# Two tiles for the high and the low part of every moving operand of the feed-forwards, the low ones at another place in a 256-byte line

## The chip, the cores and the metric

One core of one Trainium2 chip runs the whole program. The time is device microseconds from start to end of the program. A profile beside it records one execution: when each engine (PE for matrix multiplies, PEld for loading their weights, DVE and ACT for elementwise work, POOL, and SP, which here issues transfers) was busy and what ended each wait.

## The reference

Two layers of a diffusion backbone over 512 latent tokens and 256 context tokens, model width 1024. Layer 0 mixes tokens by windowed attention, layer 1 by retention; after each mixer comes a SwiGLU feed-forward of inner width 2816, modulated and gated by columns made from a condition vector. In layer 1 only the latent tokens go through the feed-forward. Cut to what matters here:

```python
D_MODEL = 1024; SEQ = 512; CTX_LEN = 256
D_FF = -(-8 * D_MODEL // (3 * 256)) * 256

def swiglu(h, w_in, w_out):
    gate, up = jnp.split(h @ w_in, 2, axis=-1)
    return (jax.nn.silu(gate) * up) @ w_out

    for i in range(DEPTH):
        mx = jnp.split(c_act @ ada_w[i] + ada_b[i], 6, axis=-1)
        mc = jnp.split(cc_act @ ada_w[i] + ada_b[i], 6, axis=-1)
        ...  # the mixer, with its gated residual
        x = x + mx[5] * swiglu(modulate(rms_norm(x, norm2_g[i]), mx[3], mx[4]), ffn_w_in[i], ffn_w_out[i])
        if need_ctx_out:
            y_ctx = y_ctx + mc[5] * swiglu(modulate(rms_norm(y_ctx, norm2_g[i]), mc[3], mc[4]),
                                           ffn_w_in[i], ffn_w_out[i])
```

## The kernel before

**Tokens lie along the columns.** A tile has 128 partitions, which hold 128 of the 1024 features, and its columns are tokens. Weights are the stationary operand of a matmul, tokens or activations the moving one.

**Every matmul comes in threes.** A 32-bit value is split into a high part, rounded by a cast on ACT (`fp32r`), and a low part, the rest, by a subtraction on DVE (`split`, L164). A product is then the sum of three matmuls into the same PSUM tile: weights high times tokens high, weights low times tokens high, weights high times tokens low. `mm3` (L144) issues them at L148, L149 and L150; `product` (L902) does the same in a loop at L908. So one matmul in three reads the low part of a moving tile.

**Layer 0's feed-forward** (L923 to L1157) treats 512 latent and 256 context tokens as 768, in two halves of 384 columns (`THIRDS`). It runs over 22 blocks of 128 inner features. The first two (`first_two`, `plain`) multiply each half by the gate and the up weights, 8 steps of `mm3` each. The other 20 (`seven`, L1025) use a Strassen-like scheme: seven products of 4 steps, each 384 columns wide, on sums of halves made once (`token_sums`, `last_sum`). Blocks are gathered in groups of 2, 4, 4, 4, 4, 4 (`FFN_GROUPS`), and after the first block of the next group `output` (L1078) multiplies the group's activations by the output weights: for each of 8 output tiles one sum over the latent tokens (512 columns, PSUM tile pj) and one over the context tokens (256 columns, PSUM tile Z).

The moving tiles are `aq` (768 columns: high part first, low part behind it, 384 each; 8 in pool `ep`, 20 in pool `hq`) and `act` (1536 columns: 768 high, 768 low; 5 in `ep`). `parts` (L927) cuts an `aq` in two. Before the first use, the `act` tiles hold the unsplit tokens (`tm`), two per tile. Of the 20 `aq` tiles in `hq`, 12 serve for a short while as room for weight blocks of 512 columns: `unit` (L1107) loads two blocks of modulation weights, `unit(10)` and `unit(11)`, each as 8 transfers of 512 columns (four of the second go to another tile, `crow`), and `ada_unit` (L302) multiplies them at L308 in pieces of 128 columns. After that `token_sums` fills the same tiles with the sums of halves.

**Layer 1's feed-forward** (L1610 to L1723) has 512 latent tokens in two halves of 256 columns. The first three blocks are plain, the other 19 go through its own `seven` with seven products of 4 steps, 256 columns wide. Moving tiles: `hx` (the tokens, 8 high and 8 low, allocated in turn in pool `hX`), `sA` (sums of halves, likewise, pool `fp`), both 512 columns, and `ax` (activations, 512 columns, in turn, 10 in pool `fa`), which `output` (L1686) reads whole, 512 columns per matmul, 8 output tiles x 22 blocks.

**Where a tile starts in a 256-byte line.** Nearly all tiles have a multiple of 64 columns (256 bytes), so they start at byte 0 of a line, but the program shifts some with a small padding tile: `off_grid(pool, cols)` (L225) allocates `cols` columns of 4 bytes in the pool and clears them on POOL. 16 columns shift what follows by 64 bytes, 48 by 192. Worked out from the sizes of the tiles that stand ahead, the starts are:

| moving tile | columns read | before, high / low | after, high / low |
|---|---|---|---|
| aq (layer 0) | 384 | 0 / 0 | 0 / 64 |
| act (layer 0) | 512 and 256 | 0 / 0 | 0 / 64 |
| hx, sA (layer 1) | 256 | 64 / 64 | 64 / 192 |
| ax (layer 1) | 512 | 0 / 0 | 0 / 192 |
| h (layer 0's mixer) | 512 | 0 / 0 | the same |
| hc (layer 0's mixer, context) | 256 | 192 / 192 | the same |
| qk, wx, aq, hc, sA in layer 1's mixer | 256, 512 | 0 / 0 | the same |

The weights (`whi`, `wlo` and the tiles that stand in for them) start at byte 0 of a line in both feed-forwards, before and after.

**What sets the order.** Instructions stand on each engine in an order that a planner chooses from the program as written, its dependencies and its own costs; each engine then works through its list in order. SP issues nearly all transfers, weights above all, one after the other, and a transfer into a tile waits until the tile's last reader is done. Tiles of one tag take turns in their buffers.

## Time and profile before

| | |
|---|---|
| time, median of 3 runs | 1767.8 us (1767.19 to 1768.53) |
| the profiled execution | 1765.14 us |
| its span, first to last instruction | 1763.4 us |
| mean granted TensorE clock | 0.996 of full speed |
| PE busy | 1716.5 us, 97% of the span |
| DVE busy | 1332.7 us, 76% |
| ACT busy | 841.3 us, 48% |
| layer 0's feed-forward, by the chain | from about 375 to 900 us |
| layer 1's feed-forward | from about 1409 us to the end |

How to read it: busy times are unions of the instructions' intervals, and those of PE are modelled at their ends: neighbouring matmuls overlap in the record (a 256-column matmul has a duration of about 0.28 us and starts 0.12 us after the one before). The distance between starts is what a stream of matmuls costs. The chain of waits merges neighbours on one line into one row, with start, length and count, and so gives that distance. Names are those of the program with buffer numbers left out: `Y<-aq,whi` is a matmul into PSUM tile Y that reads moving tile aq and weights whi.

### The profile page before, as it was taken

To read this page: it belongs to the slowest core of one execution; us is meant where nothing else is said; L and a number is where in the kernel's file an instruction comes from. 1 tells how busy PE (TensorE), PEld (TensorE's weight loads), DVE (VectorE), ACT (ScalarE), POOL (GpSimd) and SP (SyncE) were. 2 spreads that over 40 slices of the span, in tenths; PEclk is the share of its full clock that TensorE was granted. 3 is DMA by queue.
4 is the path that set the end of the run, shared out by engine and by line. 5 is a ranking of instruction groups with operands and counts; after the bars stand their busy time and mean duration, and the time that the engine had idled before them with its cause. 6 is when DMAs were issued, how large, how long until landed. Compare 5 with 4: busy or idle time off the path is not lost.

```text
span 1763.4 us, 27889 instructions
## 1 busy us (share of the span) xinstructions
PE 1716.5 (97%) x10984; PEld 1531.5 (87%) x10984; DVE 1332.7 (76%) x2342; ACT 841.3 (48%) x1487; POOL 122.4 (7%) x267
## 2 busy tenths in 40 slices
PE   6999999999999999999998999999999999999999
PEld 4788787889999999999887888898897889989998
DVE  6687786478778787877799758758767897777774
ACT  5467786364434333343464534524534565345442
POOL 0014344000000000000010000000000100000000
PEclk9999999999999999999999999999999999999999
DMA  9510014133243434343333434434433323233322
GB/s 345 232 49 14 15 58 157 49 127 113 96 132 122 142 120 155 108 145 130 96 133 120 157 98 132 155 108 133 146 105 108 96 93 111 85 108 108 97 83 84
DMA packets 60899, 205.65 MB, mean 117 GB/s; under 512 B 6752, under 2 KB 7136, under 8 KB 60640
## 3 DMA queue, kind: packets, MB, share of 16 engines
q1 hardware_dynamic: 53856, 178.71, 30.5%
q0 software_dynamic: 6912, 25.17, 4.5%
q8 instruction: 86, 1.41, 0.3%
q14 instruction: 45, 0.37, 0.1%
HBM read 201.75 MB, written 2.10 MB: 116 GB/s over the span
## 4 chain that ended last, share of the span: by engine, by line
PE 78%; DVE 12%; DMA 5%; ACT 3%; issue 1%; POOL 0%; SPq 0%; DVEq 0%; ACTq 0%; POOLq 0%
PE Y L908 14%; PE Z L908 7%; PE pj L150 7%; PE pj L149 7%; PE pj L148 7%; DMA wraw<-in_wst_dram 4%; PE X L908 3%; PE Y L1253 3%; PE Z L1266 3%; DVE wlo L166 3%; PE pO L732 2%; PE pT L704 2%; PE S L684 2%; PE pj L1266 2%; PE X L1253 1%
## 5 line engine op out<-in xcount | busy, mean ns | idle before, releaser
L165 ACT CAST whi<-wraw 128x1024 fp32r<-128x1024 f32 x177 | 185.5, 1051 | 305.2 <-PE Z L150 71.5
L166 DVE TENSOR_TENSOR wlo<-wraw,whi 128x1024 fp32r<-128x1024 f32 x177 | 216.1, 1223 | 39.4 <-ACT whi L165 38.9
L908 PE MATMUL Y<-aq,whi 128*128 128x384 f32 x640 | 173.9, 335 | 0.4 <-ACT hn L1046 0.3
L253 DVE SCALAR_TENSOR_TENSOR res<-pj,mod,res 128x512 f32<-128x512 f32 (+1 forms) x110 | 80.4, 732 | 81.2 <-PE pj L150 80.1
L141 DVE TENSOR_TENSOR wlo<-wraw,whi 128x1024 fp32r<-128x1024 f32 x79 | 96.5, 1223 | 35.2 <-ACT whi L140 34.6
L140 ACT CAST whi<-wraw 128x1024 fp32r<-128x1024 f32 x79 | 82.9, 1049 | 77.1 <-PE Z L150 24.3
L908 PEld LDWEIGHTS Y<-aq,whi 128*128 128x128 f32 x640 | 116.7, 188 | 1.8 <-ACT hn L1046 1.4
L908 PE MATMUL Y<-aq,wlo 128*128 128x384 f32 x320 | 107.0, 334 | 0.0
L271 DVE CUSTOM_DVE_ANT_0 y<-adaw,crow,small_sb 128x1024 bf16<-128x1024 f32 x64 | 81.9, 1280 | 32.9 <-DMA adaw<-in_adaT_dram 32.7
L1266 PE MATMUL Z<-whi,sA 128*128 128x512 f32 x256 | 81.0, 392 | 1.4 <-ACT whi L165 1.4
L101 ACT ACTIVATE pr<-pr,stat,qs 128x513 f32<-128x513 f32 (+2 forms) x96 | 74.2, 775 | 12.4 <-DVE stat L691 9.7
L698 POOL TENSOR_SCALAR pr<-pr,stat 128x512 f32<-128x512 f32 (+2 forms) x96 | 65.3, 693 | 76.6 <-DVE stat L695 57.7
L148 PE MATMUL pj<-ax,whi 128*128 128x512 f32 x176 | 68.7, 390 | 1.2 <-DVE res L253 1.2
L150 PE MATMUL pj<-ax,whi 128*128 128x512 f32 x176 | 68.7, 390 | 0.0
L149 PE MATMUL pj<-ax,wlo 128*128 128x512 f32 x176 | 68.5, 389 | 0.0
L148 PE MATMUL pj<-act,whi 128*128 128x512 f32 x168 | 66.0, 393 | 0.0
L149 PE MATMUL pj<-act,wlo 128*128 128x512 f32 x168 | 65.9, 392 | 0.0
L150 PE MATMUL pj<-act,whi 128*128 128x512 f32 x168 | 65.5, 390 | 0.0
L268 POOL DMA_DIRECT2D adaw<-in_adaT_dram x48 | 25.6, 533 | 514.6 <-DVE mod L271 420.1
L908 PE MATMUL Y<-sA,whi 128*128 128x256 f32 x304 | 60.8, 282 | 0.0
L908 PEld LDWEIGHTS Y<-aq,wlo 128*128 128x128 f32 x320 | 60.1, 188 | 0.0
L685 DVE CUSTOM_DVE_ANT_0 pr<-S,mask,qs 128x256 f32<-128x256 f32 (+1 forms) x96 | 52.5, 568 | 8.4 <-PE S L684 5.1
(545 smaller groups left out, 5227.8 us busy)
## 6 DMA issues: line engine op xcount, KB each, us to landing
wraw<-in_wst_dram SPq DMA_DIRECT2D x238, 512.0 KB, 3.6
adaw<-in_adaT_dram POOLq DMA_DIRECT2D x48, 512.0 KB, 3.8
wx<-in_wst_dram SPq DMA_DIRECT2D x24, 512.0 KB, 4.9
adan<-in_adaQ_dram SPq DMA_DIRECT2D x16, 512.0 KB, 8.4
adan<-in_adaN_dram SPq DMA_DIRECT2D x16, 512.0 KB, 7.5
res<-in_xT_dram SPq DMA_DIRECT2D x16, 256.0 KB, 4.4
q<-in_adaN_dram SPq DMA_DIRECT2D x16, 256.0 KB, 3.2
aq<-in_adaN_dram SPq DMA_DIRECT2D x12, 256.0 KB, 5.9
```

The source lines that it names most:

```text
L101: ins = nc.scalar.activation(*args, **kw)
L140: nc.scalar.copy(hi, raw)
L141: nc.vector.tensor_tensor(lo, raw, hi, op=sub)
L148: nc.tensor.matmul(o, whi, xhi, start=first, stop=False)
L149: nc.tensor.matmul(o, wlo, xhi, start=False, stop=False)
L150: return nc.tensor.matmul(o, whi, xlo, start=False, stop=last)
L165: nc.scalar.copy(hi, t)
L166: return nc.vector.tensor_tensor(lo, t, hi, op=sub)
L253: return nc.vector.scalar_tensor_tensor(res[d], o, mods[l, s][:, part, d:d + 1], res[d], mult, add)
L271: after(nc.vector.tensor_tensor_reduce(junk, w, cr[:, s * 1024:(s + 1) * 1024], 1.0, sm_t[:, C_ADAB + l * 48 + j:C_ADAB + l * 48 + j + 1], ...
L908: nc.tensor.matmul(o, p, r, start=first and k + i == 0, stop=k == 3 and i == 2, skip_group_check=not first)
L1266: ins = nc.tensor.matmul(o, p, r, start=first and k + i == 0, stop=k == 3 and i == 2, skip_group_check=not first)
```

## The change

Each moving operand of the feed-forwards that was one tile, or two tiles allocated in turn, becomes two tiles with tags of their own: `aqh` and `aql`, `acth` and `actl`, `hxh` and `hxl`, `sAh` and `sAl`, `axh` and `axl`. All high tiles of a tag lie together, then comes a padding tile, then all low tiles, then a padding that completes the line. The number of buffers stays the same. What moves in the line stands in the table above: the low parts alone. A weight block that `unit` loads now spans a high tile (384 columns) and the first 128 columns of a low tile, so it takes two transfers; the function `cut` gives its four pieces to `ada_unit`. `sh2` grows from 16 to 64 columns so that it fills a line.

```diff
@@ -292,12 +292,15 @@
 
 
 
+    def cut(t):
+        return [t[:, j * P:(j + 1) * P] for j in range(4)]
+
     def unit_load(u):
         w = []
         for kk in range(4):
             w.append(T(st_p, 1024, "adan", 8))
             nc.sync.dma_start(w[kk], adaN[u, kk])
-        return [t[:, a * 512:(a + 1) * 512] for t in w for a in range(2)]
+        return [cut(t[:, a * 512:(a + 1) * 512]) for t in w for a in range(2)]
 
     def ada_unit(u, w, bank=pT, ccol=ccol):
 
@@ -305,7 +308,7 @@
         o = bank()[:, 0:P]
         for k in range(KT):
             for j in range(4):
-                nc.tensor.matmul(o[32 * j:32 * j + 32, :], ccol[:, k, :], w[k][:, j * P:(j + 1) * P],
+                nc.tensor.matmul(o[32 * j:32 * j + 32, :], ccol[:, k, :], w[k][j],
                                  start=k == 0, stop=k == KT - 1)
         rows = t_sq(P)
         nc.scalar.copy(rows, o)
@@ -795,7 +798,7 @@
     def load_streams():
         streams.extend(((0, load_stream(0)), (1, load_stream(1))))
 
-    def cut(w):
+    def cut_w(w):
         return [tuple(t[:, k * P:(k + 1) * P] for t in w) for k in range(KT)]
 
     def key_room_w():
@@ -846,7 +849,7 @@
 
     ends = []
     end = lambda: ends.pop(0)()
-    weight = lambda room=None: wo.append(room() if room else cut(next_w(ap, 1)))
+    weight = lambda room=None: wo.append(room() if room else cut_w(next_w(ap, 1)))
     steps = {}
     for g in range(NKV - 1):
         a, b = make_q(2 * g + 2), make_q(2 * g + 3)
@@ -889,7 +892,7 @@
     ep = E.enter_context(tc.tile_pool(name="ep", bufs=1, reuse_waits="tile"))
     wo_p = A.enter_context(tc.tile_pool(name="wo", bufs=1, reuse_waits="tile"))
     for wsel[0] in (0, 2, 3, 1):
-        wo.append(cut(next_w(wo_p)))
+        wo.append(cut_w(next_w(wo_p)))
     (_, xr), (_, cres) = streams
     for s, d in WO_ORDER:
         out_part(s, d, 0, KT)
@@ -923,13 +926,26 @@
     Q = ExitStack()
     hq = Q.enter_context(tc.tile_pool(name="hq", bufs=1, reuse_waits="tile", side="right"))
     fp = F.enter_context(tc.tile_pool(name="fp", bufs=1, reuse_waits="tile"))
-    quarter = lambda: T(hq, 768, "aq", 20, F32R)
-    parts = lambda t: (t[:, 0:384], t[:, 384:768])
+    def quarter(dt=F32R):
+        hi = T(hq, 384, "aqh", 20, dt)
+        if not begun:
+            off_grid(hq, 16)
+        lo = T(hq, 384, "aql", 20, dt)
+        if not begun:
+            begun.append(off_grid(hq, 48))
+        return hi, lo
+
+    begun = []
     bank = lambda n: T(psF, 512, n, 2)[:, 0:384]
-    fp32 = [T(ep, 2 * WIDE, "act", 5) for _ in range(4)]
-    tm = [fp32[k % 4][:, k // 4 * WIDE:(k // 4 + 1) * WIDE] for k in range(KT)]
-    A = {(k, 0): parts(T(ep, 768, "aq", 8, F32R)) for k in range(KT)}
-    A.update({(k, 1): parts(quarter()) for k in range(KT)})
+    tm = [T(ep, WIDE, "acth", 5) for _ in range(4)]
+    A = {(k, 0): [T(ep, 384, "aqh", 8, F32R)] for k in range(KT)}
+    off_grid(ep, 16)
+    tm += [T(ep, WIDE, "actl", 5) for _ in range(4)]
+    for k in range(KT):
+        A[k, 0].append(T(ep, 384, "aql", 8, F32R))
+    off_grid(ep, 48)
+    A[0, 1] = quarter()
+    A.update({(k, 1): quarter() for k in range(1, KT)})
 
     def latent_shape():
 
@@ -962,12 +978,12 @@
             nc.vector.tensor_tensor(t1[:, h1], t2[:, h2], t1[:, h1], op=sub)
             nc.vector.tensor_tensor(park[:, k * 384:(k + 1) * 384], t2[:, h1], t1[:, h1], op=sub)
             for n, t in ((1, t2[:, h2]), (3, t1[:, h2]), (2, t1[:, h1])):
-                S[n, k] = parts(quarter())
+                S[n, k] = quarter()
                 split(t, *S[n, k])
 
     def last_sum():
         for k in range(4):
-            S[4, k] = parts(quarter())
+            S[4, k] = quarter()
             split(park[:, k * 384:(k + 1) * 384], *S[4, k])
 
     S = {}
@@ -975,12 +991,12 @@
                **{n: (lambda k, n=n: S[n, k]) for n in (1, 2, 3, 4)}}
 
     def new_act():
-        return T(ep, 2 * WIDE, "act", 5, F32R)
+        return T(ep, WIDE, "acth", 5, F32R), T(ep, WIDE, "actl", 5, F32R)
 
     def finish_half(a, i, t, up):
         nc.vector.tensor_tensor(t, t, up, op=mult)
         c = THIRDS[i]
-        return split(t, a[:, c], a[:, c.start + WIDE:c.stop + WIDE])
+        return split(t, a[0][:, c], a[1][:, c])
 
     def project_half(w, i, tag):
         o = bank(tag)
@@ -1088,7 +1104,7 @@
             for k in range(gsz):
                 c0 = k * nd * P + (d % nd) * P
                 mm3(o, (wd[0][:, c0:c0 + P], wd[1][:, c0:c0 + P]),
-                    (acts[k][:, c], acts[k][:, c.start + WIDE:c.stop + WIDE]), k == 0, k == gsz - 1)
+                    (acts[k][0][:, c], acts[k][1][:, c]), k == 0, k == gsz - 1)
             ins = gated_add(s, 0, 5, d, o, res)
             if cr and not final and s == 0 and d % 2:
                 ada_next(ins)
@@ -1105,12 +1121,18 @@
                     one(*st, d)
 
     def unit(u):
-        w = [T(hq, 768, "aq", 20)[:, 0:512] for _ in range(KT - 4 * (u == 11))]
-        if u == 11:
-            more = T(fp, 2048, "crow", 1)
-            w += [more[:, i * 512:(i + 1) * 512] for i in range(4)]
+        more = T(fp, 2048, "crow", 1) if u == 11 else None
+        w = []
         for k in range(KT):
-            nc.sync.dma_start(w[k], adaN[u, k // 2][:, k % 2 * 512:k % 2 * 512 + 512])
+            src = adaN[u, k // 2][:, k % 2 * 512:k % 2 * 512 + 512]
+            if k >= KT - 4 and more:
+                w.append(cut(more[:, (k - 4) * 512:(k - 3) * 512]))
+                nc.sync.dma_start(more[:, (k - 4) * 512:(k - 3) * 512], src)
+                continue
+            a, b = quarter(F32)
+            nc.sync.dma_start(a, src[:, 0:384])
+            nc.sync.dma_start(b[:, 0:P], src[:, 384:512])
+            w.append([a[:, 0:P], a[:, P:2 * P], a[:, 2 * P:], b[:, 0:P]])
         return ada_unit(u, w, pj, columns)
 
     ada_q = []
@@ -1573,8 +1595,11 @@
         hW_parts = lambda: (T(hW, 1024, "whi", 2, F32R), T(hW, 1024, "wlo", 2, F32R))
         hm = [T(hM, 512, "hm", 8) for _ in range(KT)]
         off_grid(hX, 16)
-        hx = [(T(hX, 512, "hx", 16, F32R), T(hX, 512, "hx", 16, F32R)) for _ in range(KT)]
-        off_grid(hX, 48)
+        hx = [[T(hX, 512, "hxh", 8, F32R)] for _ in range(KT)]
+        off_grid(hX, 32)
+        for pair in hx:
+            pair.append(T(hX, 512, "hxl", 8, F32R))
+        off_grid(hX, 80)
         done = []
 
         def second_norm(k, c, behind=()):
@@ -1614,13 +1639,24 @@
     fp = F.enter_context(tc.tile_pool(name="fp", bufs=1, reuse_waits="tile"))
     ring += [rp, rp, hW, hW, fp, fp]
     wsel[0] = 4
-    sh2 = T(fp, 16, "sh2", 1)
-    sA = [(T(fp, 512, "sA", 16, F32R), T(fp, 512, "sA", 16, F32R)) for _ in range(KT)]
-    off_grid(fp, 48)
+    sh2 = T(fp, 64, "sh2", 1)
+    off_grid(fp, 16)
+    sA = [[T(fp, 512, "sAh", 8, F32R)] for _ in range(KT)]
+    off_grid(fp, 32)
+    for pair in sA:
+        pair.append(T(fp, 512, "sAl", 8, F32R))
+    off_grid(fp, 80)
+    begun = []
     operand_a = operands(lambda k, half: [a[:, HALVES[half]] for a in hx[k]], sA)
 
     def new_act():
-        return T(fa, 512, "ax", 10, F32R), T(fa, 512, "ax", 10, F32R)
+        hi = T(fa, 512, "axh", 5, F32R)
+        if not begun:
+            off_grid(fa, 48)
+        lo = T(fa, 512, "axl", 5, F32R)
+        if not begun:
+            begun.append(off_grid(fa, 16))
+        return hi, lo
 
     def half(i):
         return [(a[:, HALVES[i]], b[:, HALVES[i]]) for a, b in hx]
```

## The prediction

> **What bounds the kernel now.** I read the page's busy times first, then the stages of the two feed-forwards, then the chain that ended last, and there the distance from one matmul to the next. In the window view the columns are the stretch, its length, and the busy time of PE, PEld, DVE, ACT and POOL.
>
> ```profile
> span 1763.4 us, 27889 instructions
> PE 1716.5 (97%) x10984; PEld 1531.5 (87%) x10984; DVE 1332.7 (76%) x2342; ACT 841.3 (48%) x1487; POOL 122.4 (7%) x267
> ...
> 447.00:505.00 58.00, 58.00 (x336) 57.84 (x335) 43.66 (x65) 27.27 (x45) 2.65 (x5) 1.00 0.34 111
> 540.00:597.00 57.00, 57.00 (x330) 56.96 (x329) 47.63 (x72) 26.93 (x45) 4.22 (x8) 1.00 0.45 141
> 1461.00:1500.00 39.00, 38.98 (x327) 38.61 (x326) 29.60 (x41) 22.26 (x40) 0.00 (x0) 1.00 0.39 123
> 1522.00:1562.00 40.00, 39.47 (x333) 39.20 (x332) 27.37 (x39) 21.88 (x40) 0.00 (x0) 1.00 0.35 107
> ```
>
> Inside both feed-forwards (first two windows: layer 0, last two: layer 1) PE is busy without a gap at a granted clock of 1.00, and DVE, the next engine, has at least a sixth of its time free (47.63 of 57). So what a matmul costs here is the distance between the starts of two neighbours; the durations of single matmuls overlap and say nothing. The chain and the timeline give these starts (us, length, what):
>
> ```profile
> 640.62 2.08 PE Z L908 x12
> 642.70 4.16 PE Y L908 x24
> ...
> 1395.91 0.12 PE pj L149
> 1399.99 0.12 PE Y L150
> ...
> 1461.65 1.41 PE Z L908 x12
> 1468.85 2.83 PE Y L908 x24
> ...
> 321.06 0.28 PE L149 MATMUL S<-hc,wlo 128*128 128x256 f32 x1
> 323.56 0.28 PE L150 MATMUL S<-hc,whi 128*128 128x256 f32 x1
> ...
> 98.44 0.12 PE pj L148
> 100.91 0.12 PE pj L148
> ...
> 1453.57 0.23 PE pj L149
> 1461.30 0.23 PE pj L150
> ...
> 505.06 0.23 PE pj L148
> 507.14 0.23 PE pj L148
> ```
>
> I divide each stretch by its number of steps. 384 columns, moving tile at byte 0 of a line (aq): 4.16/24 = 173.3 ns. 256 columns at byte 0 (qk, 34 steps): 4.08/34 = 120.0. 256 columns at byte 64 (hx, sA): 2.83/24 = 117.9 and 1.41/12 = 117.5, so 117.8. 256 columns at byte 192 (hc) comes in two kinds: 2.50/22 = 113.6 in one run, 2.47/21 = 117.6 in another. 512 columns at byte 0 (ax, 34 steps): 7.73/34 = 227.4; right after a switch from the 384-column stream (act, 9 steps) 2.08/9 = 231.1. From 256 to 384 to 512 columns the distance grows by 53.3 and 54.1 ns, so what a matmul costs on top of its columns is about the same for all three sizes, and I carry a difference seen at 256 columns over to the others. All weights lie at byte 0 in these rows. That the three 256-column distances differ by where the moving tile starts, 120.0, 117.8 and 113.6 to 117.6, is the evidence the forecast rests on; it is one stage against another, not an experiment.
>
> **The change part by part.** No matmul is added or removed, and each keeps its shape. High tiles stay where they were (byte 0 in layer 0 and for ax, 64 for hx and sA). A third of the matmuls, those at L150 or the last of the three in a product, read the low tile, which moves.
>
> Layer 0, byte 0 to byte 64. From the loops: 20 fast products of 7x4 steps give 560 low matmuls, two plain blocks of 2x2x8 give 64, all 384 columns wide; the output sums give 22x8 = 176 at 512 and 176 at 256 columns. That is 976 low matmuls. Price: 120.0 - 117.8 = 2.2 ns each, 976 x 2.2 = 2.15 us. Ends: nothing, if the 64-byte rows are fast for a reason of their stage, and 6.4 ns each (120.0 - 113.6), 6.2 us. I take 2.2, which is the row for just this start.
>
> Layer 1, hx and sA low, byte 64 to byte 192. 19 products x 28 steps = 532, three plain blocks x 2x2x8 = 96: 628 at 256 columns. Price between 117.8 - 117.6 = 0.2 and 117.8 - 113.6 = 4.2 ns; nothing in the rows says which kind of run this will be, so half way, 2.1 ns: 1.3 us (0.1 to 2.6).
>
> Layer 1, ax low, byte 0 to byte 192. 176 at 512 columns, 120.0 - 117.6 = 2.4 to 6.4 ns, half way 4.4: 0.8 us (0.4 to 1.1).
>
> The high matmuls I price at nothing: around the two changes of moving start that the rows show (192 bytes after 0 at 98.44, 64 after 0 behind 1461.30) the distance is at once that of the new tile, so it goes with a matmul's own start. What speaks against: nowhere in this trace does the start alternate in every triple, as it will.
>
> On the other side: two transfers per weight block in the modulation units.
>
> ```profile
> 387.24 7.58 SPq L1113 DMA_DIRECT2D aq<-in_adaN_dram  x12
> 406.01 5.27 SPq L122 DMA_DIRECT2D wraw<-in_wst_dram  x3
> DMA to landing us min/median/max: 2.7/5.4/6.6
> 410.93 3.63 PE pj L308 x128
> 411.38 0.75 POOL L268 DMA_DIRECT2D adaw<-in_adaT_dram  x1 [94.53 <-PE pj L308]
> 1406.45 0.40 DVE res L1553
> 1406.85 0.39 DVE hx L243
> 1448.88 1.14 DVE wlo L166
> 1453.07 0.50 PE pj L148
> ```
>
> Twelve issues take 7.58 us on SP's queue; 24 take 15.2, so the last goes out at 402.4 and lands by 409.0, before its readers start at 410.93. Behind them on that queue stands the weight load of 406.01, still 3.6 us away. So nothing, with 1.9 us of cover; were landing as much later again as its own spread (6.6 - 2.7 = 3.9), PE would stand 2 us, once. Nine more memsets go to POOL, which has been idle for 94.5 us when its next work comes; none of them stands before anything in layer 1 that PE reads. Each new pool's padding has to wait for its space, as the tiles beside it do. Casts and subtractions write to another byte of the line: hx, at byte 64, took 0.39 us for 256 columns on DVE, an operation of the same size on res, at byte 0 of the line, 0.40, so nothing. At the start of layer 1's feed-forward, where DVE sets the pace up to 1453.07, the planner places some casts, splits and output matmuls one step earlier or later; one DVE step is 1.14 us, so I bound this by 1.1 us either way and take zero.
>
> Sum: -2.15 - 1.3 - 0.8 = -4.2 us, all on PE's path, since the windows leave no gap in which it could be lost. The profiled execution took 1765.14 us (span 1763.4 and 1.7 around it), 2.7 below the median of 1767.8. Off the median: **1763.6 us**.
>
> **A rule against it.** The rows show that 256 columns cost 113.6 to 120.0 ns with the same weights' start. The Trainium skill, "TensorE: Matmul & The Clock Gate", section "Step-by-step: what each phase is for", says that PE reads the moving tile and the weights through two independent ports, so that loading weights takes nothing from a running matmul, and gives (section "Back-to-back issue gap") a distance of columns over 2.4 GHz plus 2.5 ns, in which no address stands. By that rule the change would be worth nothing and the time 1767.8. The trace disagrees with the figure (an estimate from that page, 109.2 ns at 256 columns, stands against 113.6 to 120.0), so its rule for addresses weighs little with me.
>
> **The rivals.**
> *No effect.* The differences belong to the stages (which weights, which PSUM tile, what DVE does meanwhile), not to the start in the line. For it: the byte-192 runs are 113.6 and 117.6 at the same start. Against it: three stages with byte 64 or 192 all lie below every long run at byte 0. Time 1767.8.
> *The neighbour decides.* What costs is that the next stream begins at the same place in the line as the one before or as its weights; then both borders of every triple gain, at best down to the 113.6 row. Layer 0: 976 x 2 x 6.4 = 12.5 us; layer 1: 628 x 2 x 4.2 = 5.3 and 176 x 2 x 6.4 = 2.3. Together 20.1: 1747.7. For it: the two kinds of byte-192 runs show that more than the own start counts. Against it: long runs at one start are not the slowest there are.
> *Slower: each change of start costs.* After the switch to another stream at 505.06 the steps are 231.1 instead of 227.4, 3.7 ns more, for a while. If alternating starts keep PE in that condition, both matmuls that follow a border pay: 1,780 triples x 2 x 3.7 = 13.2 us, less the 4.2: +9.0, 1776.8. It decides from 4.2/3560 = 1.2 ns a border. Against it: at 98.44 and 1461.65 a change of start cost nothing that shows; but the switch there happens once.
>
> **How the numbers follow.** Own start decides 0.42 (range of its own 1758 to 1767, by the ends above), neighbour 0.20, no effect 0.16, slower 0.22. A fifth of a per cent, 3.5 us, is about what a measurement of this kernel can tell from no change. Of the first case I put 0.06 inside that, of no effect all but 0.01, of slower 0.01: faster 0.56, within 0.22, slower 0.22. The range 1747 to 1773 leaves out the better part of the slower case beyond half its price and a tail of the neighbour case.
>
> **What would show it.** Right: sums of 384 columns at 2.07 us for twelve instead of 2.08, 256-column sums of layer 1 at 1.39 to 1.41 instead of 1.41, everything outside the feed-forwards as it was. Neighbour: 384-column twelves near 2.03 and 1.38 in layer 1. Slower: twelves above 2.10. A PE gap before 410.9 would be the transfers. Most likely to make the forecast wrong is the high matmuls' share, which I set to zero: one nanosecond on each of the 3,560 is 3.6 us.

## The result, and the profile after

The changed kernel took 1773.31 us in the median of 20 runs, the kernel before 1768.38 us in 20 runs beside it: a ratio of 1.0024 (95% interval 1.0017 to 1.0032), slower by about 4.2 us (3.0 to 5.7). The forecast was 1763.6 us and faster; the time moved the other way and lies just above the range (1747 to 1773).

Part 1 of the page of the changed kernel:

```profile
span 1767.3 us, 27919 instructions
PE 1717.7 (97%) x10984; PEld 1529.9 (87%) x10984; DVE 1333.9 (75%) x2342; ACT 840.4 (48%) x1487; POOL 123.4 (7%) x276
```

The number of matmuls is the same; POOL has nine instructions more. The page of the profile hardly tells the two kernels apart. The profiled execution of before was 2.7 us below its median and this one, 1769.4 us, 3.9 below its own, so the spans can't be subtracted either. What can be compared are distances and single waits. The chain that ended last, changed kernel, in layer 0 (384 columns, then 512) and layer 1 (256); columns are start, length, what:

```profile
641.53 4.17 PE Y L911 x24
645.71 2.09 PE X L911 x12
...
871.81 0.23 PE pj L150
...
880.16 0.23 PE pj L150
...
1471.45 1.40 PE Z L911 x12
1472.86 2.81 PE Y L911 x24
```

The same view of the kernel before, at the 512-column rows (the others stand in the prediction):

```profile
871.90 0.23 PE pj L149
...
880.29 0.23 PE pj L150
```

384 columns: 4.17 us for 24 instead of 4.16. 256 columns of layer 1: 2.81 instead of 2.83. 512 columns: 36 steps in 8.35 us, 231.9 ns, where before 37 steps took 8.39 us, 226.8 ns. The twelves of layer 1 are as forecast for the case taken (1.39 to 1.41), those of layer 0 are not (2.07 was said); and the 512-column matmuls lost five nanoseconds here, for which the sum had no term.

The second place is the start of layer 1's feed-forward. The window view over 64.10 us from the first matmul on hx, before and after (two fences, same columns as in the prediction):

```profile
1409.70:1473.80 64.10, 60.82 (x453) 57.20 (x452) 59.80 (x101) 35.92 (x59) 1.66 (x2) 1.00 0.26 83
```

```profile
1411.93:1476.03 64.10, 58.89 (x441) 55.35 (x440) 58.34 (x97) 33.88 (x56) 3.78 (x8) 1.00 0.27 83
```

PE gets through 441 matmuls instead of 453 in the same time and is busy for 1.9 us less. POOL is the one engine that has more to do in it: 8 instructions instead of 2. Its timeline in the kernel before (start, length, what, and in brackets the idle time before it):

```profile
1405.97 0.26 POOL L227 MEMSET off<- 128x16 f32 x3
1407.44 0.79 POOL L210 TENSOR_TENSOR y<-y,sq 128x256 f32<-128x256 f32 x1 [1.22 <-ACT sq L209]
1408.68 0.83 POOL L210 TENSOR_TENSOR y<-y,sq 128x256 f32<-128x256 f32 x1 [0.45 <-ACT sq L209]
```

and in the changed one:

```profile
1408.19 0.32 POOL L227 MEMSET off<- 128x16 f32 x4
1412.16 0.34 POOL L227 MEMSET off<- 128x32 f32 x2 [3.65 <-PE Y L150]
1412.47 3.58 POOL L210 TENSOR_TENSOR y<-y,sq 128x256 f32<-128x256 f32 x4
```

Before, the clearing of the padding waits for nothing, and the four additions of the norm (L210, squares of the tokens summed over features) run one by one as ACT delivers them. After, the 32-column padding between sA's high and low tiles lies on space that PE reads until about 1412.1; its clearing waits 3.65 us, and the four additions stand behind it on POOL and run in one block. The view of ACT's waits of the changed kernel, 1400 to 1425 us, shows who pays:

```profile
ACT sq L209 <- POOL y L210: 2.1, 1, 2.1
```

The transfers of the modulation units, in the timeline of SP's queue (the first, the last, and the weight load behind them):

```profile
385.11 1.20 SPq L1133 DMA_DIRECT2D aqh<-in_adaN_dram  x2
...
396.45 0.43 SPq L1134 DMA_DIRECT2D aql<-in_adaN_dram  x1
403.88 5.41 SPq L122 DMA_DIRECT2D wraw<-in_wst_dram  x3
```

24 issues take 11.8 us where 12 took 7.58, and the weight load behind them goes out 7 us after the last of them. They cost nothing that can be seen.

### The profile page after: what moved, and what is told of

It is laid out like the page before. It is cut to its first block, busy times and chain, and to the rows that moved or that the text cites. A ratio compares the mean times of both kernels' runs of the same rounds, so it can differ in the third digit from the quotient of the medians.

```text
span 1767.3 us, 27919 instructions
## 1 busy us (share of the span) xinstructions
PE 1717.7 (97%) x10984; PEld 1529.9 (87%) x10984; DVE 1333.9 (75%) x2342; ACT 840.4 (48%) x1487; POOL 123.4 (7%) x276
## 3 DMA queue, kind: packets, MB, share of 16 engines
q8 instruction: 86, 1.41, 0.3%
## 4 chain that ended last, share of the span: by engine, by line
PE 79%; DVE 12%; DMA 4%; ACT 3%; issue 2%; POOL 0%; SPq 0%; DVEq 0%; ACTq 0%; POOLq 0%
PE Y L911 15%; PE Z L911 8%; PE pj L150 7%; PE pj L149 7%; PE pj L148 7%; PE X L911 4%; DMA wraw<-in_wst_dram 4%; PE Z L1288 3%; PE pO L735 2%; PE pT L707 2%; PE S L687 2%; DVE wlo L166 2%; PE Y L1275 2%; PE X L1275 1%; PE pj L1288 1%
## 5 line engine op out<-in xcount | busy, mean ns | idle before, releaser
L911 PE MATMUL Y<-aqh,whi 128*128 128x384 f32 x320 | 108.2, 338 | 0.8 <-ACT hn L1062 0.6
L911 PE MATMUL Y<-aqh,wlo 128*128 128x384 f32 x320 | 107.9, 337 | 0.0
L911 PE MATMUL Y<-aql,whi 128*128 128x384 f32 x320 | 107.3, 335 | 0.0
L148 PE MATMUL pj<-axh,whi 128*128 128x512 f32 x176 | 68.8, 391 | 1.7 <-DVE res L253 1.7
L150 PE MATMUL pj<-axl,whi 128*128 128x512 f32 x176 | 69.2, 393 | 0.0
L149 PE MATMUL pj<-axh,wlo 128*128 128x512 f32 x176 | 68.8, 391 | 0.0
L148 PE MATMUL pj<-acth,whi 128*128 128x512 f32 x168 | 66.6, 396 | 0.0
L150 PE MATMUL pj<-actl,whi 128*128 128x512 f32 x168 | 66.1, 393 | 0.0
L149 PE MATMUL pj<-acth,wlo 128*128 128x512 f32 x168 | 66.0, 393 | 0.0
L911 PEld LDWEIGHTS Y<-aqh,whi 128*128 128x128 f32 x320 | 60.2, 188 | 1.9 <-ACT hn L1062 1.3
```

Of the source, the lines that this page charges most:

```text
L148: nc.tensor.matmul(o, whi, xhi, start=first, stop=False)
L149: nc.tensor.matmul(o, wlo, xhi, start=False, stop=False)
L150: return nc.tensor.matmul(o, whi, xlo, start=False, stop=last)
L911: nc.tensor.matmul(o, p, r, start=first and k + i == 0, stop=k == 3 and i == 2, skip_group_check=not first)
```

## The experiments

Each kernel was timed against the kernel before on the same chip. Starts are given as high/low byte in the 256-byte line. A distance is the mean, over all matmuls of a kind in its stage, of the step from one's start to the start of the next matmul in the trace; steps more than 15 ns above the median, which are waits or fall into one of the few stretches at a granted clock of 0.50 that every trace has (3.4 or 6.8 us each), are left out. In the variants with split tiles a helper `pad(pool, cols, tag)` does what `off_grid` does and is left out for zero columns.

### First: the split alone, layer 0 alone, and one start for all three matmuls

`s0_split`, `f1_layer0`, `u64` and `u192` have the split tiles and double transfers of the change and differ from it in padding alone. One place of each, layer 0's `hq`:

```diff
 # s0_split: no padding (0/0); hx, sA 64/64; ax 0/0
-            off_grid(hq, 16)
+            pad(hq, 0, "off_b")
 # f1_layer0: layer 0 as changed (0/64); layer 1 as before
+            pad(hq, 16, "off_b")
 # u64: 64/64 for aq, act, ax; 192/192 for hx, sA
+            pad(hq, 16, "off_a")
 # u192: 192/192 for aq, act, ax; 0/0 for hx, sA
+            pad(hq, 48, "off_a")
```

> The changed kernel with all paddings set so that high and low parts start where they did before (aq, act and ax at byte 0, hx and sA at byte 64); the tiles stay split and the two transfers per weight block stay. Theory 'alternating starts cost' : the matmul distances fall back to those of the kernel before (384 columns 173.4 ns, act at 512 columns 229, ax 227 to 228, hx and sA 117.8), so layer 0's feed-forward is 1.8 us shorter than in the changed kernel and the whole time is within 0.1% of the kernel before, apart from the first 20 us of layer 1's feed-forward. Rival 'the split itself costs' (planner's order, transfers, waits): the time stays 3 to 4 us above the kernel before, and the 1.5 us that the changed kernel lost in the first 20 us of layer 1's feed-forward are lost here too.

> The changed kernel's starts in layer 0's feed-forward alone (aq and act 0 high, 64 low); layer 1's tiles split, but started as before (64 and 64, ax 0 and 0). Theory 'alternating starts cost': layer 0 as in the changed kernel, so 384 columns at 174.0 ns on average and act at 512 columns at 231.5, together 1.8 us more between the first fast product and the start of layer 1; layer 1's ax back to 227 to 228 and its 256-column distance at 117.8. Time 1 to 3 us above the kernel before. Rival 'only layer 1 matters': no more than 0.5 us in layer 0.

> High and low parts at the same start, but another than before: aq, act and ax at byte 64, hx and sA at byte 192. Theory 'own start' (the prediction's): aq 173.4 - 2.2 = 171.2 ns, act and ax at 512 columns 2.2 less than at byte 0 (226.8 and 225.2), act at 256 columns 117.8, hx and sA 113.6 to 117.6; the time 4 to 12 us below the kernel before. Rival 'only 256 columns gain from the start': act at 256 columns 117.8, but 384 and 512 columns 173.4, 229 and 227.5 as at byte 0, and the time about 1 us below to 1 us above. Rival 'starts off byte 0 cost at wide matmuls': 384 and 512 columns above 174 and 231.

> High and low parts at the same start: aq, act and ax at byte 192, hx and sA at byte 0. Theory 'own start': aq down to 167 to 171 ns, ax and act at 512 columns 2.4 to 6.4 below byte 0, act at 256 columns 113.6 to 117.6, hx and sA up to 120.0 (1,876 x 2.2 = 4.1 us lost there), so the time 3 to 12 us below the kernel before. Rival 'only 256 columns gain': 384 and 512 columns as at byte 0, the time about 3 us above the kernel before because of hx and sA at byte 0.

Measured: s0_split 1.0014 (1.0001 to 1.0027), f1_layer0 1.0021 (1.0011 to 1.0031), u64 1.0002 (0.9991 to 1.0014), u192 1.0058 (1.0045 to 1.0071). The distances in ns, with two kernels of later sets:

| stream | before | changed | u64 | u128 | u192 | swap |
|---|---|---|---|---|---|---|
| layer 0, 384 columns (1680) | 173.4 (0/0) | 174.0 (0/64) | 173.3 | 176.0 | 173.7 | 174.1 (64/0) |
| layer 0, 512 (528) | 229.0 (0/0) | 231.5 (0/64) | 228.9 | 233.0 | 233.0 | 233.1 (64/0) |
| layer 0, 256 (528) | 119.4 (0/0) | 118.2 (0/64) | 116.9 | 118.5 | 114.0 | 118.1 (64/0) |
| layer 1, 256 (1884) | 117.8 (64/64) | 117.5 (64/192) | 115.5 (192/192) | 119.0 | 119.9 (0/0) | 117.8 (192/64) |
| layer 1, 512 (528) | 227.1 (0/0) | 229.2 (0/192) | 229.1 (64/64) | 233.0 | 233.5 | 233.3 (64/0) |

In brackets the number of matmuls, and the starts where the kernel's name doesn't give them. s0_split and f1_layer0 agree with before or with the changed kernel in every cell to 0.3 ns. In layer 1's 256 columns, though, 0.3 ns is all that the change shows: s0_split, with the old starts, has 117.5 there as well, and `control` of the second set, the kernel before once more, 117.6. The scatter comes in stretches. Nearly all steps of these traces have 117.8 ns in the mean, but 60 in a row take 113.3 in control (1469.2 to 1476.0 us), and s0_split has such stretches too, at byte 64 (its chain; twelve in 1.49 us with a wait, then twelve in 1.37):

```profile
1543.74 1.49 PE Y L916 x12
1545.24 1.37 PE X L916 x12
```

At byte 192 (u64) half of the steps are of the short kind, in before none, in control 5%. So a mean at 256 columns is, at these two places, a mixture of two paces, and the start shifts the mixture. The chain of u192, in the stretch of 512 columns shown above:

```profile
871.96 0.24 PE pj L150
...
881.76 0.24 PE pj L150
```

42 steps in 9.80 us, 233.3 ns: at 512 columns byte 192 costs 6.5 ns in this stretch (4.0 in the mean of the stage), where the forecast had it gain. At 256 columns it gains 5.4 (119.4 to 114.0). So the price of a start depends on the width, and changes its sign with it. And two starts that cost the same alone (layer 0, 512 columns: 229.0 at byte 0, 228.9 at byte 64) cost 231.5 when they alternate: there is a price on the change of start too.

### Second: does the split cost anything, and does the 256-column gain arrive?

`control` is the kernel before, unchanged. `b_192` is the kernel before, unsplit, with only the 256-column streams moved, on all three matmuls. `split0` and `split1` split the tiles of one layer with all starts as before.

```diff
 # b_192: act 64/64, hx and sA 192/192
+    off_grid(ep, 16)
     fp32 = [T(ep, 2 * WIDE, "act", 5) for _ in range(4)]
+    off_grid(ep, 48)
...
-        off_grid(hX, 16)
+        off_grid(hX, 48)
         hx = [(T(hX, 512, "hx", 16, F32R), T(hX, 512, "hx", 16, F32R)) for _ in range(KT)]
-        off_grid(hX, 48)
+        off_grid(hX, 16)
...
-    sh2 = T(fp, 16, "sh2", 1)
+    sh2 = T(fp, 48, "sh2", 1)
 # split1: only layer 1's tiles, no start moved
+        hx = [[T(hX, 512, "hxh", 8, F32R)] for _ in range(KT)]
+            pair.append(T(hX, 512, "hxl", 8, F32R))
 # split0: only layer 0's, with two transfers for a block
+        hi = T(hq, 384, "aqh", 20, dt)
+        lo = T(hq, 384, "aql", 20, dt)
```

> The kernel before once more, unchanged, as a second arm beside itself. Every theory expects a ratio of 1.000; how far it is off, and how wide its interval is, is how far the other ratios can be trusted. If it comes out near 1.0014, the 2.5 us that the split tiles with the old starts showed is nothing but scatter.

> The kernel before with its tiles unsplit, but the 256-column streams off byte 0 on all three matmuls: act at byte 64 (high and low), hx and sA at byte 192 (high and low); aq and ax stay at byte 0. Width theory (only 256 columns gain, by the own start): 528 matmuls on act from 119.4 to 116.9 ns and 1884 on hx and sA from 117.8 to 115.2 ns, the other distances unchanged: -1.3 and -4.8 us, ratio 0.9966. The theory that the gain at 256 columns is lost again somewhere else (the same distances gave only 1.0002 with split tiles, where -2.9 us were expected by the spacing): 0.999 to 1.001. If splitting itself costs about 2.5 us, this kernel shows the gain in full.

> Only layer 0's tiles split (with two transfers per modulation block), no start changed, layer 1 as before. If the splitting costs time there (transfers, order): 1.001 to 1.002 and the distances as before. If it costs in layer 1: 1.000.

> Only layer 1's tiles split (hx, sA, ax into tiles of their own), no start changed, layer 0 as before. If the order at the start of layer 1's feed-forward costs: 1.001 to 1.002 and a longer stretch between 1405 and 1455 us. If the cost lies in layer 0 or is scatter: 1.000.

Measured: control 0.9995 (0.9987 to 1.0004), split0 0.9997 (0.9988 to 1.0006), split1 0.9998 (0.9989 to 1.0007). Splitting one layer costs nothing that shows, transfers included; the 1.0014 of s0_split, whose interval begins at 1.0001, is best taken as scatter: its runs had a mean granted clock of 0.9936, those of before beside it 0.9943, and the means of the two sets of times differ by 1.1 us only.

b_192 came to 0.9993 (0.9982 to 1.0003), though its distances fell nearly as expected: 117.4 ns in layer 0, 115.6 in layer 1, together 5.2 us. The chain of b_192 in layer 1 shows where part of it went:

```profile
1530.03 1.41 PE Y L908 x12
...
1551.19 1.36 PE Z L908 x12
1552.55 2.73 PE Y L908 x24
...
1555.30 1.24 DVE wlo L141
...
1556.55 4.57 DMA wraw<-in_wst_dram
...
1561.20 1.05 ACT whi L140
1562.26 0.31 ACT hn L107
1562.57 0.27 ACT res L1677
...
1562.88 1.68 PE Y L908 x12
```

The control at the same place:

```profile
1558.25 1.41 PE Z L908 x12
1559.67 1.41 PE Y L908 x12
1561.08 1.41 PE X L908 x12
1562.49 1.41 PE Y L908 x12
```

In the control PE follows on PE. In b_192 a raw weight block could not be fetched until DVE had freed its buffer (1556.5) and took 4.57 us to land; ACT's cast of that block (`whi`) holds up ACT's copy that frees PSUM tile Y, and PE stands for 0.97 us at this one matmul and 0.23 us at four others. The shorter twelves are only part of the reason, for the profiled execution of the kernel before waits at the same place by the same chain:

```profile
1550.55 1.43 PE Y L908 x12
...
1553.36 1.24 DVE wlo L141
...
1554.61 4.61 DMA wraw<-in_wst_dram
...
1559.30 1.05 ACT whi L140
...
1560.97 1.68 PE Y L908 x12
```

PE stands for 0.69 us there at the old pace, and for 0.91 us in s0_split, whose block takes 4.84 us to land; in the control the cast starts 3.6 us after the issue, and nothing waits. So whether this weight is late depends first on how long its transfer takes, and at the longer landing there is no room even at 1.41 us. Behind the start of the stage the shorter distances of b_192 are worth 3.3 us, and these five waits take 1.9 us. The first 450 matmuls of the stage gain nothing (64.1 us from the first to the 451st in b_192, 64.05 in the control), since DVE sets the pace there; that loses another 0.9.

### Third: layer 1 alone, the starts exchanged, and one more weight buffer

```diff
 # f2_layer1: layer 0 all at byte 0, layer 1 as changed
+            pad(hq, 0, "off_b")
 # swap: high and low starts exchanged (aq, act, ax 64/0; hx, sA 192/64)
+            pad(hq, 16, "off_a")
+            pad(hq, 48, "off_b")
 # ring5, b_ring5: the kernel before, and b_192, with five raw buffers in turn
+    def raw5():
+        nraw[0] += 1
+        return w_raw(fp, 3) if nraw[0] % 5 in (0, 1, 3) else w_raw()
...
-        g, u = w_raw(fp, 2), w_raw()
+        g, u = raw5(), raw5()
...
-                w.append(next_w(fp, 4))
+                w.append(next_w(fp, 4, raw5()))
```

> The change in layer 1's feed-forward alone (hx, sA 64/192, ax 0/192); layer 0's tiles are split but all start at byte 0 as before. By the distances that the whole change showed there: 1884 matmuls of 256 columns 0.2 to 0.3 ns shorter (-0.5 us), 528 of 512 columns 2.05 ns longer (+1.1 us): ratio 1.0003. If the 1.5 us that the whole change lost in the wait at the start of this feed-forward belong to these starts: 1.0012. The recorded prediction for this half of the change was -2.1 us: 0.9988.

> The starts of the change the other way round in layer 0 (high at byte 64, low at byte 0) and layer 1 (hx, sA 192/64; ax 64/0), so that two matmuls in three read the moved start. Own start with a price for each width: act at 512 columns 229.0 ns (both starts are 229.0 alone), 384 columns 173.4, act at 256 columns (2x116.9+119.4)/3 = 117.7, hx and sA (2x115.2+117.8)/3 = 116.1, ax (2x229.1+227.05)/3 = 228.4: together -0.9 - 3.2 + 0.7 = -3.4 us, less what a late weight takes back in layer 1. Border theory (the change of start inside a triple costs by itself): act 231.5 and 384 columns 174.0 as in the whole change, 256 columns of layer 1 near 117.5: together about +2 us, 1.001.

> The kernel before, all starts as before, with five instead of four buffers for the raw weights of layer 1's feed-forward, used in turn (three in fp, two in rp), so that a weight block can be loaded one block earlier. If the weights are not late at the old distances: 0.9995 to 1.0005, with the same distances and no shorter sum. If they were already late: 0.998 to 0.9995.

> The kernel with act at byte 64 and hx, sA at byte 192 on all three matmuls (unsplit, the one that gave 0.9993 where its distances promised 0.9966) and the same five buffers for raw weights. Theory of the late weight (the 256-column gain of layer 1 is taken back by a weight block that arrives after PE is ready, 1.0 us at one matmul in that kernel): the wait is gone and the ratio is 0.997 to 0.998. If the gain is lost otherwise (half clock, other waits): 0.999 as without the fifth buffer.

Measured: f2_layer1 1.0017 (1.0009 to 1.0026), swap 1.0036 (1.0023 to 1.0049), ring5 0.9999 (0.9990 to 1.0007), b_ring5 0.9992 (0.9983 to 1.0001).

swap decides between the own start and the border, most clearly in layer 0. The chain of swap there, and in the second fence that of u64:

```profile
871.81 0.23 PE pj L150
...
881.84 0.23 PE pj L148
```

```profile
871.81 0.23 PE pj L150
...
881.88 0.23 PE pj L149
```

43 steps in 10.03 us, 233.3 ns, where byte 0 alone has 226.8 and byte 64 alone (u64, 44 steps in 10.07 us) 228.9. In layer 1 the 256 columns at 192/64 cost 117.8, as if all were at byte 64, though two in three start at 192. The change of start takes back all that the better start gives, and at 512 columns more. Not every change does: ax at 0/192 has 229.2 ns, which is what its own starts give, (2 x 227.1 + 233.5)/3 = 229.2.

ring5 takes the time of the kernel before, and neither kernel with five buffers settles what a late weight costs: they change the planner's order at the start of the stage, and PE waits 1.9 us (b_ring5: 2.6) at a matmul there, where the control waits 1.2, and 1.0 us (1.2) at a later one, where it doesn't wait. b_ring_late leaves the start alone.

### Fourth: the queued clearing, byte 128, and the late weights again

```diff
 # a_nowait: the changed kernel, two paddings of sA's pool not cleared
-    off_grid(fp, 32)
+    T(fp, 32, "off32", 1)
...
-    off_grid(fp, 80)
+    T(fp, 80, "off80", 1)
 # after_again: the changed kernel, no edit
 # u128: 128/128 everywhere
+            pad(hq, 32, "off_a")
 # b_ring_late: b_ring5, with the turn only from the eighth block on
+        if f < 7:
+            return w_raw(fp, 3) if own else w_raw()
```

> The changed kernel without the two clearings of padding in sA's pool (32 and 80 columns, cleared on POOL; the padding stays, so every start is as changed). Theory of the queued clearing: in the changed kernel the first of the two waits 3.6 us for PE at the start of layer 1's feed-forward, four additions of the norm stand behind it on POOL and ACT waits 2.1 us for them; without it the additions come as before and the time is 1.2 to 1.5 us lower than the changed kernel, a ratio of about 1.0015 where the distances alone give 1.0013. Rival (the loss there comes with the starts themselves, by slower DVE or ACT operations on them): hx on DVE still 507 ns and the ratio as for the changed kernel, 1.0024.

> The changed kernel once more, unchanged, beside the kernel without the two clearings. Every theory expects 1.0017 to 1.0032 again; by the queued clearing its additions on POOL come again in one row of four behind a wait of about 3.6 us, by scatter in the profile they do not.

> All moving tiles of both feed-forwards at byte 128, high and low alike. No change of start inside a triple, so the border theory prices it by the own starts alone. If the own price goes steadily from byte 0 over 64 to 192: 256 columns 115.5 to 116.5 ns, 512 columns 229 to 233 ns, 384 columns 173.4 to 174; ratio 0.998 to 1.002. If byte 128 behaves like byte 0 (half a line): 119.5, 229 and 227, 173.4; ratio 1.001.

> Unsplit, act at byte 64, hx and sA at byte 192, the rest at byte 0, and the five raw weight buffers in turn only from the eighth block of layer 1's feed-forward on, so that the start of the stage keeps the order of the kernel before (with the five from the start, that start took 2.6 us longer). If late weights and that start are all that took the gain back: no wait of over 0.5 us behind the start and a ratio of 0.997 to 0.998. If something else gives the time back: 0.999.

Measured: after_again 1.0027 (1.0015 to 1.0039), a_nowait 1.0019 (1.0010 to 1.0028), u128 1.0065 (1.0052 to 1.0078), b_ring_late 0.9986 (0.9977 to 0.9995).

after_again repeats the wait of 3.65 us on POOL and the four additions in one block. In a_nowait they are gone (POOL's timeline):

```profile
1409.90 0.32 POOL L227 MEMSET off<- 128x16 f32 x4
1411.37 0.79 POOL L210 TENSOR_TENSOR y<-y,sq 128x256 f32<-128x256 f32 x1 [1.15 <-ACT sq L209]
1412.61 0.83 POOL L210 TENSOR_TENSOR y<-y,sq 128x256 f32<-128x256 f32 x1 [0.45 <-ACT sq L209]
```

and the window view of a_nowait over 64.10 us from the first matmul on hx is back at 455 matmuls (at a granted clock of 0.97 there):

```profile
1413.65:1477.75 64.10, 61.26 (x455) 58.26 (x454) 59.19 (x101) 35.52 (x59) 1.84 (x4) 0.97 0.27 83
```

From that matmul to the 451st it is 64.1 us before, 65.6 and 65.5 in the two traces of the changed kernel, and 63.9 here. So the clearing costs 1.5 us; the medians of the two kernels (1773.79 and 1771.62) differ by 2.2, their intervals overlap. The rival for this place, that DVE works slower on tiles with unlike starts, falls too. The group of the low part of hx, 1395 to 1445 us, in the changed kernel and in a_nowait:

```profile
L243 DVE SCALAR_TENSOR_TENSOR hxl<-hm,mod,hxh 128x256 fp32r<-128x256 f32 x16 | 7.6, 507 | 0.6 <-ACT hxh L242 0.6
```

```profile
L243 DVE SCALAR_TENSOR_TENSOR hxl<-hm,mod,hxh 128x256 fp32r<-128x256 f32 x16 | 7.2, 483 | 0.0
```

The same starts, and 483 ns again (482 before): the 507 went with the late additions, not with the starts.

u128 is the slowest kernel of all. Its chain in layer 0, 384 columns:

```profile
642.08 2.11 PE Y L916 x12
644.20 2.11 PE Z L916 x12
```

2.11 us for twelve, 176 ns: byte 128 is the worst place at 384 columns and no better than 192 at 512. The price is no steady function of the place in the line, and half a line is not like a whole one.

b_ring_late is the one version whose interval lies below 1: 0.14% faster than the kernel before, less than the 0.3% that its distances promise. Part of this may not be the kernel's: its runs had a mean granted clock of 0.9954 and those of before beside it 0.9942, and among the latter 0.001 of clock goes with 1.2 us, which is more than half of the difference of 2.5 us between the means. The start of the stage has the order and, by the distances of its matmuls, the length of before (63.95 us), so that its shorter 256-column matmuls gain nothing there; and a late weight is still there, 1.4 us at one matmul and 0.14 to 0.24 at four others, mostly at other places than in b_192. The five buffers moved the wait; they did not end it.

### All runs against their distances

The sum of (distance - distance before) x count, over 1768.6 us, beside the ratio; the 192 matmuls of 384 columns in the first two blocks are counted with their own distance. The next to last column adds 1.5 us where the clearing waits on POOL. The kernels in which no start was moved show how far such a sum scatters, 0.6 us:

| kernel | sum, us | ratio by it | with POOL's wait | measured |
|---|---|---|---|---|
| changed | +2.3 | 1.0013 | 1.0022 | 1.0024, 1.0027 |
| a_nowait | +2.3 | 1.0013 | | 1.0019 |
| f1_layer0 | +1.4 | 1.0008 | | 1.0021 |
| f2_layer1 | +0.4 | 1.0002 | 1.0011 | 1.0017 |
| swap | +5.8 | 1.0033 | 1.0041 | 1.0036 |
| u192 | +7.8 | 1.0044 | | 1.0058 |
| u128 | +11.8 | 1.0067 | | 1.0065 |
| u64 | -4.8 | 0.9973 | | 1.0002 |
| b_192 | -5.2 | 0.9970 | | 0.9993 |
| b_ring5 | -4.4 | 0.9975 | | 0.9992 |
| b_ring_late | -5.2 | 0.9971 | | 0.9986 |
| control, split0, split1 | -0.5, -0.2, 0.0 | 0.9997, 0.9999, 1.0000 | | 0.9995, 0.9997, 0.9998 |
| s0_split, ring5 | -0.6, -0.4 | 0.9997, 0.9998 | | 1.0014, 0.9999 |

What makes matmuls longer arrives in full; what makes layer 1's shorter does not, and in b_192 DVE's pace at the start and the late weights behind it take 2.8 of its 4.0 us there.

## Why the prediction was wrong

**"I carry a difference seen at 256 columns over to the others": this failed.** The evidence, that 256 columns cost 120.0, 117.8 and 113.6 to 117.6 ns by their start, was right in its sense, and u64 and u192 show it as an experiment (119.4, 116.9 and 114.0 in the same loop); but the two kinds are no property of byte 192, since byte 64 has both as well. And the rows of before had no 384- or 512-column stream off byte 0, and an overhead that is equal at the three widths does not make it equal at the other starts. Of the sum's terms: layer 0, forecast -2.15 us, measured +1.8 (384 columns +1.1, 512 columns +1.3, 256 columns -0.6). ax, forecast -0.8, measured +1.1. hx and sA, forecast -1.3, measured -0.6 against the trace of before and -0.1 against that of control, so no gain is shown.

**"The high matmuls I price at nothing": this failed too, and weighs about as much.** With the prices of one start for all three matmuls (the table of the first set) the change would have come to about -0.9 us; so of the 6.5 us between the forecast -4.2 and the measured +2.3, the price carried over makes 3.3 and the alternation 3.2. In layer 0 the starts 0 and 64 cost the same alone at 384 and 512 columns in the mean of all matmuls, and alternating costs 2.5 ns more at 512 columns (528 matmuls: 1.3 us) and 0.6 at 384 (1680: 1.0 us). The two changes of start that the rows of before showed cost nothing, but each happened once, between 256- and 512-column streams at other starts. The prediction named this as what would most likely make it wrong. The rival "each change of start costs" came nearest: 3.7 ns on each of two borders of a triple is 2.5 ns in the mean over three, which is what 512 columns pay. In the 512-column stream of layer 0 the step behind L148, L149 and L150 grew by 3.9, 0.7 and 2.9 ns, so the two matmuls that follow a border pay; in swap it is 2.1, 2.1 and 8.0, for which that rule does not account. Its 9 us came from charging all widths alike; 384 columns pay a quarter of it, and at 256 columns the change of start only takes back a gain.

**"None of them stands before anything in layer 1 that PE reads": wrong, 1.5 us.** Nine memsets were priced by their own length on an idle engine. One of them waits for its space, and POOL's queue is in order, so the wait was passed on to the four additions behind it, from there to ACT (2.1 us) and to PE. The row with POOL's long idle time ("94.53") was from another stage; the additions at 1402 to 1412 us stand in the timeline of before and were left out of the argument. The Trainium skill, "PSUM — Partial Sum Buffer", section "Engine vs sequencer instructions", says that the queues of ScalarE, VectorE and GpSimdE are strict FIFO; the trace agrees, with 3.65 us of waiting ahead of the additions in both traces of the changed kernel. That the padding "has to wait for its space" was seen, and the question who stands behind it was not asked.

**"All on PE's path, since the windows leave no gap in which it could be lost": wrong for layer 1**, though it did not decide here. The first three windows show no gap; the fourth has PE busy for 39.47 of 40.00 us, and the half microsecond that is missing is the late weight at 1560.97 shown above. It was read as no gap. And a full window can't show how far away the next wait is: b_192 stands longer there, and at four more places.

**Right:** the transfers (hidden, as said, and their issue shorter than estimated: 11.8 us instead of 15.2); the split of either layer and the planner's reordering (split0 and split1 within 0.03% of no change); the distances outside the feed-forwards stayed as they were (in layer 1's mixer 226.7 ns for 512 columns of qk and 119.9 for 256 of aq, in both traces).

**The rule against the change.** In the formula of the Trainium skill, "TensorE: Matmul & The Clock Gate", section "Back-to-back issue gap", no address enters, and by it the time would have been that of before. The section calls this formula the gap of an isolated matmul and says that in a stream of weight loads and matmuls both set the distance; the prediction held it against such a stream. The forecast gave it little weight, because the distances of before disagree. They do, and more so now: the same loop at the same width runs at 114.0 to 119.4 ns (layer 0) or 115.5 to 119.9 (layer 1) at 256 columns and at 227.1 to 233.5 at 512, by the starts alone. But disagreeing with a rule of no effect is no evidence for the sign of the effect.

**Open:** up to 1 us of the time lost (the distances and POOL's wait make 3.8, the two timings say 4.2 and 4.8; f1_layer0, without POOL's wait, lies 2.3 us above its distances, beyond its interval, and a_nowait 1.1, within it). s0_split, f1_layer0 and u192, timed in one set against the same 21 runs of before, all lie 2 to 3 us above their distances (two of them at a lower mean granted clock, 0.9936 against 0.9943), u128 of another set does not; whether the split of both layers together has a small price that neither half shows could not be resolved. Why the price depends on start and width as it does was not tried, nor was whether 256 bytes is the length that matters: all kernels move starts in steps of 64 bytes within it.

## What to carry to other kernels

A price seen at one operand width and one pattern is a price for that width and pattern; before it is carried over, one kernel with all operands at one start and one with them exchanged tells own price, border price and sign apart. An instruction added to an idle in-order engine costs its wait, not its length, to all that stands behind it: look up what it waits for and who comes next at that place, not elsewhere in the profile. And a window in which the leading engine never waits tells that nothing else is slower, not by how much, and one execution doesn't stand for all: the same kernel waited 0.69 us for a weight in one trace and not at all in another.

## What the runs showed of the hardware

- The mean distance of a matmul with a new weight load each time depends on the byte in a 256-byte line at which its moving tile starts, by up to 6.4 ns, in opposite senses at 256 columns (119.4 to 119.9 at byte 0, 116.9 to 117.8 at 64, 118.5 to 119.0 at 128, 114.0 to 116.0 at 192) and at 512 (227.1 to 229.0, 228.9 to 229.1, 233.0, 233.0 to 233.5); 384 columns pay at byte 128 (176.0 against 173.3 to 173.7), and in the first two blocks at 192 (176.5 against 173.5).
- Alternating between bytes 0 and 64 brings 512 columns to 231.9 ns (two in three at byte 0) or 233.3 (two in three at 64) in a stretch where the two alone have 226.8 and 228.9; between 0 and 192, with two in three at 0, nothing beyond the mean of the two shows (229.2).
- A 256-column stream off byte 0 has two paces, and keeps one for dozens to hundreds of matmuls: in b_192 twelve take 1.41 us at 1530.03 and 1.36 at 1551.19, the same tiles at the same starts, and in s0_split, at byte 64, 1.37 at 1545.24. At byte 192 about half of layer 1's steps have the shorter one (u64, b_192), at byte 64 none to 7%, at byte 0 hardly any (u192). The two kinds in the prediction (113.6 and 117.6) are these two paces; what sets the pace was not tried.
